# Attention outputs leave their PSUM bank in one copy and are added when the rows are loaded; seven bias tables are added up on GpSimd

## The chip, the cores and the metric

The kernel runs on one core of one Trainium2 chip. Its time is the device time of one execution in microseconds. Three runs of the kernel before took 1325.66 to 1327.61 us, median 1326.53 us. A further execution was recorded by the hardware profiler; all lines of the profile come from that one. The engines are named as the profile names them: PE (TensorE, with PEld for its weight loads), DVE (VectorE), ACT (ScalarE), POOL (GpSimd) and SP (SyncE, whose queue issues the DMAs).

## The reference

One layer of an encoder on 1024 tokens of 1024 features, in float32:

```
h = rms_norm(x) ; q_a,k_a,v_a, q_b,k_b,v_b, g_a,g_b = split(h @ w_in)
o_a = neighbourhood_attention(norm(q_a), norm(k_a), v_a, rpb)   # 8 heads of 64, 8 x 16 window of a 16 x 64 grid, bias by relative place
o_b = sliding_window_attention(norm(q_b), norm(k_b), v_b, sink, t5)  # 8 heads, 2 key heads, +-128 tokens
y = sigmoid(g_a) * (o_a @ w_branch_a) + sigmoid(g_b) * (o_b @ w_branch_b)
x = x + y @ w_out
x = x + (silu(rms_norm(x) @ w_gate) * (rms_norm(x) @ w_up)) @ w_down      # 2816 hidden
```

## The kernel before

Every operand of a product is split into a high part that TensorE's fp32r type holds and the low part that is left. A product is then three matmuls (high by high, high by low, low by high). The helper `split` makes the parts: ScalarE copies the high part (L50), VectorE, or at some weights GpSimd, subtracts it from the source (L51; L54 where a scale goes in).

**Stages.** The projections of the first group of heads end at about 53 us of the span. Attention follows until about 398 us, then eight pairs of gate products (`gate_pair`, `Seven`) until about 524 us, then the two branch products with the sigmoids of the gates until about 611 us, then the output product and the feed-forward part.

**Attention.** There are 16 heads with 8 blocks of 128 queries each. They come in groups, two neighbourhood heads (`na`) or four sliding-window heads (`sw`): na, sw, na, sw, na, na. A loop of steps (L722 to L742) gives TensorE, for one block after another: `scores` (matmuls into a bank `s`, L592 and L593), three steps later `flip` (three transposes into a bank `t`, L616), five steps later `values` (L654). Between them go "filler" products that other stages need: the projections of the next groups (`pj`, L325 to L327) and the first gates (`pg`, L427 to L429). The order of TensorE's instructions is written out by hand.

In `scores`, VectorE adds the bias table to the scores and reduces them to their maximum (L598), ScalarE takes exponentials and their sum (L604), VectorE the reciprocal (L605), and GpSimd multiplies (L606); the result is the tile `E`. In `flip`, the transposed weights `tp` are split into `ph` (ScalarE, L50) and `pl` (VectorE, L51). In `values`, TensorE multiplies `ph` and `pl` by a tile that holds, for one head, 64 columns of the high part of the values and 64 of the low part. The result has 128 rows: 64 of one part and 64 of the other. Their sum is the head's output. It stands in the bank `o`, of which there is one (`BANKS`, L39), for half of the tokens at a time. So the product of the next half can begin only when the last half has been read out of the bank.

`store_half` (L623) reads it out: ScalarE copies 64 of the rows to the tile `of` (L636), VectorE adds the other 64 rows to them (L637). Two heads share one `of` of 128 rows, which goes to DRAM in one DMA (L640). There are 32 halves, so 32 copies, 32 adds, and 8 stores of 512 KB.

`bias_table` adds a head's relative biases (`brna`) to the window's mask (`bna`), in two adds of 128x384 for each na head (L570, VectorE). It is called two steps ahead of the head's first block, that is at the seventh block of the head before. The first head's table is made in the opening.

**Beside attention.** `row_sums` prepares operands for the gates (`ta`, `tb`, `hs`: L503, L507, L511, L515, L51, L54) during the last heads. Its instructions are held behind the instruction in `att["bound"]`, which is the latest reduction of scores (L598).

**The rows for the branch products.** `load_o` (L924 to L928) loads four tiles of 128 rows and 512 tokens from `o_dram`, one DMA each, and splits each into its parts. It is called four times, at steps of the gates 5 and 7: rows 4 to 7, first half; rows 0 to 3, first half; rows 4 to 7, second half; rows 0 to 3, second half. The first gates' values (`load_sg`) are loaded ahead of the last of these. In the turns of the branch products each pair of gates goes through a sigmoid (L993), then `product` of the weights `wb` with rows 4 to 7, then with rows 0 to 3, into banks `pb`.

**Who sets the order.** TensorE's order is the program's. The DMAs that go through `dma` (L95) keep the order of the program on SP's queue. Apart from the opening, the instructions of ScalarE, VectorE, GpSimd and the other DMAs are ordered by a scheduler.

Of the kernel before, what the change touches and what calls it, by code (L numbers as in the profile page):

```python
# [25 lines left out]
def block_kernel(ctx, tc, x, xt, small, w_in, rpb, t5, w_ba, w_bb, w_out, w_gate, w_up, w_down,  # L26
                 onehot, swmask, namask, out):
    nc = tc.nc
    P = 128
# [15 lines left out]
    def f(ap):  # L45
        return ap.bitcast(F32)

    def split(hi, lo, src, eng=None, scale=None):
        if scale is None:
            a = nc.scalar.copy(hi, src)  # L50
            b = (eng or nc.vector).tensor_tensor(lo, src, f(hi), ALU.subtract)  # L51
        else:
            a = nc.scalar.activation(hi, src, AF.Copy, scale=scale)
            b = nc.vector.scalar_tensor_tensor(lo, src, scale, f(hi), op0=ALU.mult, op1=ALU.subtract)  # L54
        return a.ins, b.ins
# [31 lines left out]
    def half_cols(h):  # L87
        return slice(h * 512, h * 512 + 512)
# [6 lines left out]
    def dma(dst, src):  # L95

        tc.keep_in_program_order(nc.sync.dma_start(dst, src))
# [4 lines left out]
    def tok(t):  # L102
        return slice(t * P, (t + 1) * P)
# [68 lines left out]
    load_small()  # L172
    load_x(0, 0, 0)

    o_dram = drp.tile([8 * P, T], F32, name="o_dram")
    swe = drp.tile([8, 512], F32, name="swe")
    nae = drp.tile([64, 744], F32, name="nae")
    g_dram = drp.tile([32 * P, 512], F32, name="g_dram")
# [47 lines left out]
    att = {}  # L226
# [205 lines left out]
    def run(gen):  # L432
        for _ in gen:
            pass
# [94 lines left out]
    with tc.tile_pool(name="at", bufs=1) as ap:  # L529
# [34 lines left out]
        def bias_table(hd):  # L564
            bt = hd["table"]
            if hd["kind"] == "sw":
                return lambda qb: bt[:, 128:384] if qb == 0 else (bt[:, 0:256] if qb == 7 else bt[:, 0:384])
            v = hd["raw"].rearrange("p (a d b) -> p d a b", a=16, d=3)
            for o in (0, 384):
                ins = nc.vector.tensor_add(  # L570
                    bt[:, o:o + 384].rearrange("p (d a b) -> p d a b", d=3, a=16), v,
                    bt[:, o:o + 384].rearrange("p (d a b) -> p d a b", d=3, a=16))
# [9 lines left out]
        of_tiles = {}  # L582

        def scores(hd, qb):
            q, k1, k2, v = groups[hd["gi"]]
# [23 lines left out]
        def flip(hd, kb):  # L609
            q0, q1 = max(0, kb - 1), min(7, kb + 1)  # L610
            n = (q1 - q0 + 1) * P
            nm_ = f"{hd['gi']}_{hd['hl']}_{kb}"
            tp = bank("t", "tp" + nm_)
            for j, qq in enumerate(range(q0, q1 + 1)):
                ko = (kb - max(0, qq - 1)) * P
                nc.tensor.transpose(tp[:, tok(j)], hd["E"][qq][:, ko:ko + P], ident)  # L616
            ph = ap.tile([P, 384], F32R, tag="ph", name="ph" + nm_, bufs=4)
            pl = ap.tile([P, 384], F32R, tag="pl", name="pl" + nm_, bufs=4)
            split(*(z[:, :n].rearrange("p (j i) -> p j i", i=P) for z in (ph, pl)),
                  tp[:, :n].rearrange("p (j i) -> p j i", i=P)[:, :, ::-1])  # L620
            hd["P"][kb] = (ph, pl)

        def store_half(hd, half):  # L623
            gi, e = hd["gi"], hd["hl"] % 2
            pair = (gi, hd["hl"] // 2)
            if pair not in of_tiles:
                of_tiles[pair] = ap.tile([P, T], F32, tag="of", name=f"of{gi}_{hd['hl']}", bufs=1)
            of = of_tiles[pair]
            own, oth = slice(e * HD, e * HD + HD), slice(HD - e * HD, 2 * HD - e * HD)
            O = hd["O"][half]  # L630
            if hd["kind"] == "na":
                dst, sh = of[own, half_cols(half)], lambda z: z
            else:
                dst = of[own, :].rearrange("p (s r c) -> p r s c", r=16, s=8)[:, 8 * half:8 * half + 8]
                sh = lambda z: z.rearrange("p (r s c) -> p r s c", r=8, s=8)
            nc.scalar.copy(dst, sh(O[oth, :]))  # L636
            nc.vector.tensor_add(dst, sh(O[own, :]), dst)  # L637
            if e == 1 and half == 1:
                row = ((0 if hd["kind"] == "na" else 4) + hd["h"] // 2) * P
                nc.sync.dma_start(o_dram[row:row + P, :], of)  # L640

        def values(hd, block):

# [115 lines left out]
    def scratch(nm):  # L759
        return hp.tile([P, 512], F32, tag="S", name=nm, bufs=2)  # L760
# [35 lines left out]
    class Seven:  # L796
# [27 lines left out]
        def step(self, p, rows=None):  # L824

            hi, lo = self.prepare(p)
            z = {1: "X", 2: "X", 5: "V", 6: "Z" if self.early else "Y", 3: "Y"}.get(p, "Z")
            ps = self.banks[z]
            for j in range(self.n) if rows is None else rows:
                bh, bl = self.mv[p][j]  # L830
                first, end = j == 0 and (p in (1, 5) or self.early and p == 3), j == self.n - 1
                nc.tensor.matmul(ps, hi[:, tok(j)], bh, start=first, stop=False, skip_group_check=True)  # L832
                nc.tensor.matmul(ps, hi[:, tok(j)], bl, start=False, stop=False, skip_group_check=True)  # L833
                nc.tensor.matmul(ps, lo[:, tok(j)], bh, start=False, stop=end, skip_group_check=True)  # L834
            if p == 1 or p == 6 and not self.early:
                nc.scalar.copy(self.banks["Z" if self.early or p == 6 else "Y"], ps)

    class TokenSums(dict):

# [84 lines left out]
    def load_o(r0, half):  # L924
        for r in range(r0, r0 + 4):
            o_rows[r, half] = hi, lo = operand("H", f"o{r}_{half}")
            dma(f(lo), o_dram[tok(r), half_cols(half)])
            split(hi, lo, f(lo))  # L928


    wb, sgs = {}, {}
# [11 lines left out]
    def load_sg(d, half):  # L943
        for br in (1, 0):
            z = sgs[d, half, br] = weight_sum(f"sg{d}_{half}_{br}")
            dma(z, gate_rows(d, br, half))
# [16 lines left out]
        load_branch(1)  # L963
        load_o(4, 1)

    def behind_three():
        load_sg(0, 0)
        load_o(0, 1)

    run(gate_pair(7, ORDER, {6: lambda: load_o(0, 0), 2: behind_two, 3: behind_three}))  # L970

    sets = bank_sets()
    my = {}
# [2 lines left out]
    def out_loads(i):  # L976
# [3 lines left out]
                w_out[0, :, tok(2 * i + a)].rearrange("(k p) c -> p k c", p=P))  # L980
        return Seven(f"o{i}", [two(z) for z in st], 4, my, sets)

    turns = [(2 * j + e, half) for j in range(4) for half in range(2) for e in range(2)]
# [535 lines left out]
```

## Time and profile before

| | |
|---|---|
| median of three runs | 1326.53 us (1325.66 to 1327.61) |
| the profiled execution | 1324.66 us |
| its span, first to last instruction | 1322.9 us |
| around the span | 1.76 us |
| PE busy | 1306.8 us (99%), 6618 matmuls |
| DVE, ACT, POOL busy | 1037.3 us (78%), 699.3 us (53%), 172.4 us (13%) |
| granted clock | 1.000 |
| DMA | 183.52 MB, 139 GB/s on average |

A row of the timeline gives the start in the span, the duration, the engine, the line, the operation, what it writes and reads, its shape, and in brackets how long the engine was idle before it and who released it. Instructions of an engine overlap a little: on VectorE the next one begins some 0.08 us before the last ends. A row of the waits gives who waited for whom, how long in total, how often, and the longest. The names leave out the buffers' numbers.

### The profile page before, as it was taken

Reading aid. Unit: us, or ns where it says so; the run is one execution under the profiler, and the core shown is the slowest. Engines: PE = TensorE matmul, PEld = TensorE weight load, DVE = VectorE, ACT = ScalarE, POOL = GpSimd, SP = SyncE. Lnnn points to the kernel's source line nnn. Section 1 sums busy time; section 2 is a strip of 40 time slices with the busy share of each in tenths; the row PEclk is TensorE's granted clock in tenths of the full one; section 3 lists DMA queues with packets and bytes.
Section 4 is the critical chain, followed back from the end, with each engine's and each line's share of the span. In section 5 each row is a group of like instructions: output and inputs, shape, how many; then the busy total and the mean of one; then the engine's idle time right before and its main releaser. Section 6 shows DMA issues by size and latency. Waiting matters only on the chain.

```text
span 1322.9 us, 19555 instructions
## 1 busy us (share of the span) xinstructions
PE 1306.8 (99%) x6618; PEld 1133.3 (86%) x6618; DVE 1037.3 (78%) x2069; ACT 699.3 (53%) x1459; POOL 172.4 (13%) x308
## 2 busy tenths in 40 slices
PE   9999999999999999999999999999999999999998
PEld 8999999999878788888887888888888888888887
DVE  5678878887787756778899887887777789798764
ACT  6667857786663334536457544434444456363532
POOL 1364645454220000000000000000000000000000
PEclk9999999999999999999999999999999999999999
DMA  9531313141424345748684532333333346672532
GB/s 311 145 88 40 92 51 94 45 118 51 130 88 167 116 138 166 250 145 259 203 290 120 159 112 80 98 118 100 92 112 119 121 167 215 239 255 64 178 129 83
DMA packets 177284, 183.52 MB, mean 139 GB/s; under 512 B 20464, under 2 KB 125936, under 8 KB 177184
## 3 DMA queue, kind: packets, MB, share of 16 engines
q1 hardware_dynamic: 176928, 182.18, 43.8%
q8 instruction: 52, 0.85, 0.3%
q14 instruction: 48, 0.39, 0.1%
q10 hardware_dynamic: 256, 0.10, 0.0%
HBM read 129.00 MB, written 48.18 MB: 134 GB/s over the span
## 4 chain that ended last, share of the span: by engine, by line
PE 84%; DVE 6%; DMA 4%; ACT 3%; issue 2%; POOL 1%; SPq 0%; ACTq 0%; DVEq 0%; POOLq 0%
PE bankZ L832 5%; PE bankZ L833 5%; PE bankZ L834 5%; PE bankY L833 5%; PE bankY L832 5%; PE bankY L834 5%; PE bankX L832 4%; PE bankX L834 4%; PE bankX L833 4%; PE pj L327 4%; PE pj L325 4%; PE pj L326 4%; PE bankV L833 3%; PE bankV L832 3%; PE bankV L834 3%; PE o L654 3%
## 5 line engine op out<-in xcount | busy, mean ns | idle before, releaser
L604 ACT ACTIVATE E<-E,nm 128x384 f32<-128x384 f32 (+3 forms) x128 | 75.7, 591 | 48.7 <-DVE nm L598 42.9
L606 POOL TENSOR_SCALAR E<-E,nm 128x384 f32<-128x384 f32 (+1 forms) x128 | 78.9, 617 | 103.8 <-DVE nm L605 72.3
L51 DVE TENSOR_TENSOR pl<-tp,ph 128x384 fp32r<-128x384 f32 (+1 forms) x128 | 66.3, 518 | 10.6 <-ACT ph L50 9.4
L50 ACT CAST ph<-tp 128x384 fp32r<-128x384 f32 (+1 forms) x128 | 57.4, 448 | 20.7 <-PE tp L616 19.6
L50 ACT CAST f<-f 128x512 fp32r<-128x512 f32 x87 | 51.3, 619 | 27.4 <-DMA f<-u_dram 22.4
L51 DVE TENSOR_TENSOR f<-f 128x512 fp32r<-128x512 f32 x87 | 56.5, 686 | 8.8 <-ACT f L50 8.7
L616 PE MATMUL tp<-ident,E 128*128 128x128 f32 x352 | 59.6, 273 | 0.1
L654 PE MATMUL o<-pl,v 128*128 128x256 f32 (+2 forms) x160 | 49.2, 308 | 4.0 <-DVE pl L51 3.9
L616 PEld LDWEIGHTS tp<-ident,E 128*128 128x128 f32 x352 | 45.2, 140 | 5.2 <-POOL E L606 0.3
L345 POOL TENSOR_TENSOR ss<-ss,mhalf 128x4 f32<-128x4 f32 (+2 forms) x42 | 49.1, 1170 | 3.1
L654 PE MATMUL o<-ph,v 128*128 128x256 f32 (+2 forms) x160 | 46.2, 303 | 3.2 <-DVE of L637 3.2
L592 PE MATMUL s<-k,q 128*128 128x384 f32 (+1 forms) x128 | 46.4, 363 | 0.0
L1213 POOL TENSOR_TENSOR rs<-rs,mhalf 128x4 f32<-128x4 f32 x2 | 2.9, 1444 | 321.5 <-DVE rs L1212 321.5
L593 PE MATMUL s<-k,q 128*128 128x384 f32 (+1 forms) x128 | 41.3, 323 | 0.0
L598 DVE CUSTOM_DVE_ANT_0 E<-s,bsw,cols 128x384 f32<-128x384 f32 (+1 forms) x64 | 36.8, 576 | 2.7 <-PE s L593 2.0
L1230 ACT ACTIVATE u<-u 128x512 f32<-128x512 f32 x44 | 27.7, 630 | 19.8 <-DVE u L1229 19.8
L598 DVE CUSTOM_DVE_ANT_0 E<-s,bna 128x384 f32<-128x384 f32 (+1 forms) x64 | 33.1, 517 | 4.8 <-PE s L593 4.2
L605 DVE RECIPROCAL nm<-nm 128x1 f32<-128x1 f32 x128 | 20.2, 159 | 21.1 <-ACT E L604 19.7
L1231 DVE TENSOR_TENSOR u<-u,wide_rs 128x512 f32<-128x512 f32 x44 | 30.2, 689 | 7.4 <-ACT u L1230 6.6
L654 PEld LDWEIGHTS o<-pl,v 128*128 128x128 f32 x160 | 30.1, 188 | 6.8 <-DVE pl L51 6.1
L833 PE MATMUL bankV<-f,f_5h 128*128 128x512 f32 x88 | 34.5, 392 | 1.0 <-DVE f L54 1.0
L654 PEld LDWEIGHTS o<-ph,v 128*128 128x128 f32 x160 | 30.1, 188 | 6.1 <-DVE of L637 5.3
(1266 smaller groups left out, 4650.7 us busy)
## 6 DMA issues: line engine op xcount, KB each, us to landing
f<-u_dram SPq DMA_DIRECT2D x77, 256.0 KB
wg_s<-in_w_gate_dram SPq DMA_DIRECT2D x22, 512.0 KB
u_dram<-u SPq DMA_DIRECT2D x33, 256.0 KB
sg<-g_dram SPq DMA_DIRECT2D x32, 256.0 KB
g_dram<-go SPq DMA_DIRECT2D x24, 256.0 KB
u_dram<-tau SPq DMA_DIRECT2D x22, 256.0 KB
u_dram<-tbu SPq DMA_DIRECT2D x22, 256.0 KB
rows<-in_x_dram SPq DMA_DIRECT2D x8, 512.0 KB
```

Of the source, the lines that this page charges most:

```text
L50: a = nc.scalar.copy(hi, src)
L51: b = (eng or nc.vector).tensor_tensor(lo, src, f(hi), ALU.subtract)
L325: nc.tensor.matmul(ps[:, :384], lh, his[k][:, :384], start=(k == 0), stop=False)
L326: nc.tensor.matmul(ps[:, :384], lh, los[k][:, :384], start=False, stop=False)
L598: att["bound"] = nc.vector.tensor_tensor_reduce(E[:, :n], s[:, :n], hd["bias"](qb), -1.0, sk if sw else 1e30, ALU.add, ALU.min, nm[:, 0:1] ...
L604: nc.scalar.activation(E[:, :m], E[:, :m], AF.Exp, bias=nm[:, 0:1], scale=-1.0, accum_out=nm[:, 1:2])
L606: nc.gpsimd.tensor_scalar(E[:, :n], E[:, :n], nm[:, 1:2], 1.0, op0=ALU.mult, op1=ALU.mult)
L616: nc.tensor.transpose(tp[:, tok(j)], hd["E"][qq][:, ko:ko + P], ident)
L654: nc.tensor.matmul(hd["O"][half][:, (a - half * 4) * P:(z + 1 - half * 4) * P], v[:, kb].rearrange("p a e -> p (a e)"), pp[:, (a - q0) * P ...
L832: nc.tensor.matmul(ps, hi[:, tok(j)], bh, start=first, stop=False, skip_group_check=True)
L833: nc.tensor.matmul(ps, hi[:, tok(j)], bl, start=False, stop=False, skip_group_check=True)
L834: nc.tensor.matmul(ps, lo[:, tok(j)], bh, start=False, stop=end, skip_group_check=True)
```

## The change

`store_half` has ScalarE copy all 128 rows of the bank to a tile `of` of the head's own. The 32 adds on VectorE are gone. Each head is stored by itself, so there are 16 stores of 512 KB, and `o_dram` has twice the rows. `load_o` loads each row tile in two DMAs, one for each part of two heads' outputs, adds them on VectorE into a scratch tile `os`, and splits that: 16 more loads of 256 KB and 16 adds. The bias tables of all na heads but the first are added on GpSimd. `att["bound"]` is VectorE's half of the flip's split. The first gates are loaded at step 1 of gate pair 7 instead of step 3, and the sigmoids are held behind the last copy between banks in gate pair 7.

```diff
-    o_dram = drp.tile([8 * P, T], F32, name="o_dram")
+    o_dram = drp.tile([16 * P, T], F32, name="o_dram")
...
-                ins = nc.vector.tensor_add(
+                ins = (nc.gpsimd if hd is not heads[0] else nc.vector).tensor_tensor(
                     bt[:, o:o + 384].rearrange("p (d a b) -> p d a b", d=3, a=16), v,
-                    bt[:, o:o + 384].rearrange("p (d a b) -> p d a b", d=3, a=16))
+                    bt[:, o:o + 384].rearrange("p (d a b) -> p d a b", d=3, a=16), ALU.add)
...
-            split(*(z[:, :n].rearrange("p (j i) -> p j i", i=P) for z in (ph, pl)),
-                  tp[:, :n].rearrange("p (j i) -> p j i", i=P)[:, :, ::-1])
+            _, att["bound"] = split(*(z[:, :n].rearrange("p (j i) -> p j i", i=P) for z in (ph, pl)),
+                                    tp[:, :n].rearrange("p (j i) -> p j i", i=P)[:, :, ::-1])
...
-            nc.scalar.copy(dst, sh(O[oth, :]))
-            nc.vector.tensor_add(dst, sh(O[own, :]), dst)
-            if e == 1 and half == 1:
-                row = ((0 if hd["kind"] == "na" else 4) + hd["h"] // 2) * P
-                nc.sync.dma_start(o_dram[row:row + P, :], of)
+            if not half:
+                hd["of"] = ap.tile([P, T], F32, tag="of", name=f"of{hd['gi']}_{hd['hl']}", bufs=1)
+            of, O = hd["of"], hd["O"][half]
+            if hd["kind"] == "na":
+                nc.scalar.copy(of[:, half_cols(half)], O)
+            else:
+                nc.scalar.copy(of.rearrange("p (s r c) -> p r s c", r=16, s=8)[:, 8 * half:8 * half + 8],
+                               O.rearrange("p (r s c) -> p r s c", r=8, s=8))
+            if half:
+                nc.sync.dma_start(o_dram[tok((0 if hd["kind"] == "na" else 8) + hd["h"]), :], of)
...
-            dma(f(lo), o_dram[tok(r), half_cols(half)])
-            split(hi, lo, f(lo))
+            for z, row in ((hi, 0), (lo, HD)):
+                src = o_dram[2 * r * P + row:2 * r * P + row + 1, half_cols(half)]
+                dma(f(z), bass.AP(src.tensor, src.offset, [[P * T, 2], [T, HD], [1, 512]]))
+            both = scratch(f"os{r}_{half}")
+            nc.vector.tensor_tensor(both, f(hi), f(lo), ALU.add)
+            split(hi, lo, both)
...
-    def behind_three():
-        load_sg(0, 0)
-        load_o(0, 1)
-
-    run(gate_pair(7, ORDER, {6: lambda: load_o(0, 0), 2: behind_two, 3: behind_three}))
+    run(gate_pair(7, ORDER, {1: lambda: load_sg(0, 0), 6: lambda: load_o(0, 0), 2: behind_two, 3: lambda: load_o(0, 1)}))
...
-            nc.scalar.activation(sg, sg, AF.Sigmoid)
+            with tc.issue_after(last_copy):
+                nc.scalar.activation(sg, sg, AF.Sigmoid)
```

TensorE's matmuls stand in the same order as before. On the other engines the order is another at many places; three of them follow. In the rows, `E4_1_6` is the weights tile of group 4, head 1, block 6, and `nm` its scale.

GpSimd's queue at the end of the second head of group 4, before:

```order
L606 TENSOR_SCALAR E4_1_5_4899<-E4_1_5_4899,nm4_1_5_4900 128x384
L606 TENSOR_SCALAR E4_1_6_4941<-E4_1_6_4941,nm4_1_6_4942 128x384
L606 TENSOR_SCALAR E4_1_7_4965<-E4_1_7_4965,nm4_1_7_4966 128x256
L606 TENSOR_SCALAR E5_0_0_4984<-E5_0_0_4984,nm5_0_0_4985 128x256
L606 TENSOR_SCALAR E5_0_1_5009<-E5_0_1_5009,nm5_0_1_5010 128x384
```

and now (line 605 is the old 606):

```order
L605 TENSOR_SCALAR E4_1_5_4886<-E4_1_5_4886,nm4_1_5_4887 128x384
L605 TENSOR_SCALAR E4_1_6_4928<-E4_1_6_4928,nm4_1_6_4929 128x384
L570 TENSOR_TENSOR bna6_4672<-brna6_4673,bna6_4672 128x384 x2
L605 TENSOR_SCALAR E4_1_7_4952<-E4_1_7_4952,nm4_1_7_4953 128x256
L605 TENSOR_SCALAR E5_0_0_4971<-E5_0_0_4971,nm5_0_0_4972 128x256
L605 TENSOR_SCALAR E5_0_1_4996<-E5_0_1_4996,nm5_0_1_4997 128x384
```

The next head's table stands between the normalisations of the last two blocks.

VectorE's queue at the same place, before (L278 makes the normalised `q` of the next group, L598 is the reduction of scores):

```order
L570 TENSOR_TENSOR bna6_4684<-brna6_4685,bna6_4684 128x384 x2
L51 TENSOR_TENSOR pl4_1_3_4959<-tp4_1_3_4954,ph4_1_3_4958 128x384
L278 SCALAR_TENSOR_TENSOR q5_1_4028<-tq5_4_0_4929,cols_81,q5_1_4028 64x512
L598 ISA E5_0_0_4984,nm5_0_0_4985<-s5_0_0_4981,bna6_4684 128x256
L598 ISA nm5_0_0_4985 128x1
L605 RECIPROCAL nm4_1_7_4966<-nm4_1_7_4966 128x1
L51 TENSOR_TENSOR pl4_1_4_4978<-tp4_1_4_4973,ph4_1_4_4977 128x384
```

and now (L597 is the old 598, L604 the old 605):

```order
L51 TENSOR_TENSOR pl4_1_3_4946<-tp4_1_3_4941,ph4_1_3_4945 128x384
L278 SCALAR_TENSOR_TENSOR q5_1_4018<-tq5_4_0_4916,cols_81,q5_1_4018 64x512
L604 RECIPROCAL nm4_1_7_4953<-nm4_1_7_4953 128x1
L51 TENSOR_TENSOR pl4_1_4_4965<-tp4_1_4_4960,ph4_1_4_4964 128x384
L597 ISA E5_0_0_4971,nm5_0_0_4972<-s5_0_0_4968,bna6_4672 128x256
L597 ISA nm5_0_0_4972 128x1
```

The table pair is gone, and the split `pl4_1_4` stands ahead of the first reduction that reads the new table.

VectorE's queue at the end of attention, in the last head (group 5, head 1), before:

```order
L454 TENSOR_TENSOR graw0_0_0_5453<-pg0_0_0_5324,wide_rs0_110 128x512
L54 SCALAR_TENSOR_TENSOR hs5_1_5477<-ta1_5460,cols_81,hs5_1_5477 128x512
L51 TENSOR_TENSOR pl5_1_4_5437<-tp5_1_4_5432,ph5_1_4_5436 128x384
L515 SCALAR_TENSOR_TENSOR tb1_5461<-xo1_5379,cols_81,ta1_5460 128x512
L51 TENSOR_TENSOR hs7_1_5523<-tb1_5461,hs7_1_5523 128x512
L51 TENSOR_TENSOR hs6_1_5499<-ta1_5460,hs6_1_5499 128x512
L51 TENSOR_TENSOR pl5_1_5_5471<-tp5_1_5_5466,ph5_1_5_5470 128x384
```

and now:

```order
L454 TENSOR_TENSOR graw0_0_0_5438<-pg0_0_0_5309,wide_rs0_110 128x512
L51 TENSOR_TENSOR pl5_1_4_5422<-tp5_1_4_5417,ph5_1_4_5421 128x384
L503 TENSOR_TENSOR ta1_5445<-xe1_5363 128x512
L51 TENSOR_TENSOR pl5_1_5_5456<-tp5_1_5_5451,ph5_1_5_5455 128x384
L507 SCALAR_TENSOR_TENSOR ta1_5445<-ta1_5445,cols_81,g22h_5210 128x512
L54 SCALAR_TENSOR_TENSOR hs5_1_5462<-ta1_5445,cols_81,hs5_1_5462 128x512
```

The splits `pl5_1_4` and `pl5_1_5` stand ahead of the row sums that they stood behind.

More of the change, by code (lines that the diff above doesn't have):

```diff
@@ L581, in block_kernel @@
                       for hl in range(nq)]
-        of_tiles = {}
         def scores(hd, qb):
@@ L618, in flip @@
             pl = ap.tile([P, 384], F32R, tag="pl", name="pl" + nm_, bufs=4)
-            split(*(z[:, :n].rearrange("p (j i) -> p j i", i=P) for z in (ph, pl)),
-                  tp[:, :n].rearrange("p (j i) -> p j i", i=P)[:, :, ::-1])
+            _, att["bound"] = split(*(z[:, :n].rearrange("p (j i) -> p j i", i=P) for z in (ph, pl)),
+                                    tp[:, :n].rearrange("p (j i) -> p j i", i=P)[:, :, ::-1])
             hd["P"][kb] = (ph, pl)
         def store_half(hd, half):
[L624 to L630, printed above, removed]
+            if not half:
+                hd["of"] = ap.tile([P, T], F32, tag="of", name=f"of{hd['gi']}_{hd['hl']}", bufs=1)
+            of, O = hd["of"], hd["O"][half]
             if hd["kind"] == "na":
-                dst, sh = of[own, half_cols(half)], lambda z: z
+                nc.scalar.copy(of[:, half_cols(half)], O)
             else:
[L634 to L637, printed above, removed]
-            if e == 1 and half == 1:
-                row = ((0 if hd["kind"] == "na" else 4) + hd["h"] // 2) * P
-                nc.sync.dma_start(o_dram[row:row + P, :], of)
+                nc.scalar.copy(of.rearrange("p (s r c) -> p r s c", r=16, s=8)[:, 8 * half:8 * half + 8],
+                               O.rearrange("p (r s c) -> p r s c", r=8, s=8))
+            if half:
+                nc.sync.dma_start(o_dram[tok((0 if hd["kind"] == "na" else 8) + hd["h"]), :], of)
         def values(hd, block):
@@ L835, in step @@
             if p == 1 or p == 6 and not self.early:
-                nc.scalar.copy(self.banks["Z" if self.early or p == 6 else "Y"], ps)
+                self.copied = nc.scalar.copy(self.banks["Z" if self.early or p == 6 else "Y"], ps).ins
     class TokenSums(dict):
@@ L981, in out_loads @@
         return Seven(f"o{i}", [two(z) for z in st], 4, my, sets)
+    last_copy = pairs[7].copied
     turns = [(2 * j + e, half) for j in range(4) for half in range(2) for e in range(2)]
```

## The prediction

> **What bounds the kernel now.** I read the page's head first, then a table of windows by stage, then TensorE's waits, then the timeline at the longest of them. The head and the windows (columns: length, then PE, PEld, DVE, ACT and POOL busy):
>
> ```profile
> span 1322.9 us, 19555 instructions
> ...
> PE 1306.8 (99%) x6618; PEld 1133.3 (86%) x6618; DVE 1037.3 (78%) x2069; ACT 699.3 (53%) x1459; POOL 172.4 (13%) x308
> ...
> 53.00:398.00 345.00, 336.00 (x2105) 318.64 (x2104) 277.45 (x794) 240.07 (x623) 159.33 (x288) 1.00 0.28 80
> ...
> 524.00:611.00 87.00, 87.00 (x385) 72.05 (x384) 65.85 (x102) 45.02 (x74) 0.00 (x0) 1.00 0.71 226
> ```
>
> TensorE is the bound: 1306.8 of 1322.9 us, at a granted clock of 1.00. The change gives it the same products in the same order, so it can win only from the 16.1 us in which TensorE stands. Attention (53 to 398 us) holds 345.00 - 336.00 = 9.0 of them; the branch products (524 to 611 us) hold none, so there any new wait is pure loss. Who makes TensorE wait (total, times, longest):
>
> ```profile
> PE o L654 <- DVE pl L51: 3.9, 6, 1.0
> PE o L654 <- DVE of L637: 3.2, 6, 1.1
> ...
> PE tq L299 <- DVE q L278: 0.7, 1, 0.7
> ```
>
> 7.8 of the 9.0 us are VectorE arriving late: 3.2 because the add L637 still reads the one O bank into which the next half is to be summed, 3.9 because the low part of the turned weights (pl) is late, 0.7 for a turned q. The change takes work off VectorE at these places.
>
> **Term 1, the O bank: -3.2 us.** The longest wait, and the one with the least room behind it:
>
> ```profile
> 353.70 0.58 ACT L636 COPY of<-o 64x512 f32<-64x512 f32 x1
> ...
> 355.43 0.69 DVE L637 TENSOR_TENSOR of<-o,of 64x512 f32<-64x512 f32 x1
> ...
> 356.17 0.33 PE L654 MATMUL o<-ph,v 128*128 128x128 f32 x1 [1.06 <-DVE of L637]
> ```
> ```profile
> 158.80 0.58 ACT L636 COPY of<-o 64x512 f32<-64x512 f32 x1
> ...
> 159.41 0.68 DVE L637 TENSOR_TENSOR of<-o,of 64x512 f32<-64x512 f32 x1
> ...
> 160.15 0.33 PE L654 MATMUL o<-ph,v 128*128 128x128 f32 x1 [0.25 <-DVE of L637]
> ```
>
> ScalarE is done with the bank at 354.28, TensorE stands from 356.17 - 1.06 = 355.11, and VectorE lets go only at 356.12. In the second place the same three times are 159.38, 159.90 and 160.09. With the copy as the only reader the bank is free 0.5 to 0.8 us before TensorE wants it, and all six waits go. The copy takes 128 rows in place of 64, with 512 elements in each as before; I take its 0.58 us unchanged. Bounds: 0.58 to 1.16 if rows counted; at 1.16 the first bank is still free in time, at 354.86, the second at 159.96 (0.06 late). So -3.1 to -3.2.
>
> **Term 2, late pl: -2.8 of 3.9 us.** Three of the six, each behind a different kind of work:
>
> ```profile
> 167.82 0.67 DVE L637 TENSOR_TENSOR of<-o,of 64x512 f32<-64x512 f32 x1
> 168.42 0.54 DVE L51 TENSOR_TENSOR pl<-tp,ph 128x384 fp32r<-128x384 f32 x1
> ...
> 170.36 0.56 DVE L51 TENSOR_TENSOR pl<-tp,ph 128x384 fp32r<-128x384 f32 x1
> ...
> 170.97 0.44 PE L654 MATMUL o<-pl,v 128*128 128x384 f32 x1 [0.78 <-DVE pl L51]
> ...
> 348.85 1.00 DVE L570 TENSOR_TENSOR bna<-brna,bna 128x384 f32<-128x384 f32 x2
> ...
> 349.10 1.13 POOL L606 TENSOR_SCALAR E<-E,nm 128x384 f32<-128x384 f32 x1 [2.45 <-PE s L593]
> ...
> 349.78 0.55 DVE L51 TENSOR_TENSOR pl<-tp,ph 128x384 fp32r<-128x384 f32 x1
> ...
> 350.38 0.39 PE L654 MATMUL o<-pl,v 128*128 128x256 f32 x1 [0.46 <-DVE pl L51]
> ...
> 388.57 0.73 DVE L54 SCALAR_TENSOR_TENSOR hs<-ta,cols,hs 128x512 fp32r<-128x512 f32 x1
> 389.23 0.54 DVE L51 TENSOR_TENSOR pl<-tp,ph 128x384 fp32r<-128x384 f32 x1
> ...
> 389.83 0.33 PE L654 MATMUL o<-pl,v 128*128 128x128 f32 x1 [0.97 <-DVE pl L51]
> ```
>
> At 170 an add L637 stands in the VectorE queue ahead; without it all behind moves up by 0.60 (the next instruction starts at 168.42): -0.60. At 350 the 0.93 us from the table pair's start to pl's goes to GpSimd: the whole 0.46. At 389 the row sums' hs (388.57 to 389.23) now stands behind pl: -0.66 of 0.97. The other three waits hold 3.9 - 0.78 - 0.46 - 0.97 = 1.7; I credit as large a share as these three give, 1.72 of 2.21, less a little: -1.1. Sum -2.8, between -1.7 (nothing for the other three) and -3.9.
>
> **Term 3, the turned q: -0.6 us.**
>
> ```profile
> 100.77 0.68 DVE L637 TENSOR_TENSOR of<-o,of 64x512 f32<-64x512 f32 x1
> ...
> 102.84 0.41 PE L299 MATMUL tq<-ident,qn 128*128 128x128 f32 x2 [0.70 <-DVE q L278]
> ```
>
> TensorE waits for VectorE's L278, which stands in VectorE's queue behind this add. Such an add holds the queue for 0.60 us (167.82 to 168.42 above), and without it 0.1 of 0.7 is left. Bounds 0 and -0.7.
>
> **What is added.** GpSimd gets seven tables. The nearest row is its two-input subtraction of the same 128x384, beside VectorE's row for the table itself:
>
> ```profile
> L51 POOL TENSOR_TENSOR wg_1l<-wg_0s,wg_1h 128x384 fp32r<-128x384 f32 x4 | 4.1, 1014 | 0.0
> ...
> L51 POOL TENSOR_TENSOR wg_7l<-wg_3s,wg_7h 128x384 fp32r<-128x384 f32 x4 | 4.4, 1111 | 1.1 <-ACT wg_7h L50 1.0
> ...
> L570 DVE TENSOR_TENSOR bna<-brna,bna x16: 537/548/703, 53.5 to 367.4; 128x384 f32<-128x384 f32 x16
> ...
> 346.06 0.59 POOL L606 TENSOR_SCALAR E<-E,nm 128x384 f32<-128x384 f32 x1 [6.30 <-DVE nm L605]
> ...
> 351.14 0.42 DVE L598 CUSTOM_DVE_ANT_0 E<-s,bna 128x256 f32<-128x256 f32 x1
> ...
> 351.82 0.48 POOL L606 TENSOR_SCALAR E<-E,nm 128x256 f32<-128x256 f32 x1 [1.59 <-PE tp L616]
> ...
> 352.74 0.27 PE L654 MATMUL o<-pl,v 128*128 128x128 f32 x1
> 352.86 0.51 PE L616 MATMUL tp<-ident,E 128*128 128x128 f32 x3
> ```
>
> So 2 x 1.01 = 2.0 us a table, by the row with nothing beside it. The far ends are 1.1 (VectorE's price) and 4.4 (twice 2 x 1.11, since a table reads runs of 8 elements, which no GpSimd row shows). The Trainium skill's GPSIMD Engine Reference, section 3, calls GpSimd the wrong engine for elementwise adds, 1.96 times as slow as VectorE; by that rule the 14 adds should stay on VectorE, and the sum would lack a table's gain and charge, about -6.1. 1014 over 548 ns is 1.85: the trace bears the factor out. But GpSimd is busy 13% of the span, and what decides is the gap behind a head's seventh block: the normalisation there takes 0.59 instead of 1.13 us once VectorE's pair is gone, the table runs from 349.7 to 351.7, the last block's normalisation is wanted from 351.82, and the transpose that reads it, the third of the three that begin at 352.86, starts about 353.1. GpSimd fits, with 0.8 us over. VectorE's next score reduction (351.14) waits 0.6 us for the table, and what is queued behind it waits too; but the split of the pl that TensorE wants first, at 352.74, has been put ahead of this reduction. I charge no more than one new wait of the present mean size, 3.9 / 6 = 0.65, for such a delay: **+0.65** (0 to 2). The same page (section 1, SBUF interfaces) says the two engines contend when VectorE reads two operands in SBUF. The rows agree: 1.13 us of normalisation beside L570, 0.59 without; now a VectorE split of weights may lose some 0.2 us beside a table, off the path.
>
> The stores double to 16 of 512 KB. Each waits for its copy alone and holds `of` until the next head's first copy, half a head later; I cost them at nothing. The loads double too:
>
> ```profile
> 526.13 0.91 SPq L97 DMA_DIRECT2D sg<-g_dram  x2
> 527.14 1.80 SPq L97 DMA_DIRECT2D o<-o_dram  x4
> ...
> 532.21 0.69 DVE L51 TENSOR_TENSOR o<-o 128x512 fp32r<-128x512 f32 x1 [1.80 <-ACT o L50]
> ...
> 536.00 0.69 DVE L51 TENSOR_TENSOR o<-o 128x512 fp32r<-128x512 f32 x1
> ...
> 540.07 0.39 PE L427 MATMUL pb<-o,wb00h 128*128 128x512 f32 x1
> ```
>
> This last set (rows 0 to 3, second half) is the tightest. Its last row is ready at 536.69 and wanted at 540.07: 3.4 us of cover. Eight issues take 3.6 us instead of 1.8, but the two gate loads ahead of them (0.91) now go earlier: 0.9 late. Four more adds of 0.60 us are 2.4 if none finds a gap. Together 0.9 to 3.3 of 3.4 us, so nothing reaches TensorE. The sigmoids behind the last bank copy wait for gates that lie ready; no cost seen.
>
> **The sum.** -3.2 - 2.8 - 0.6 + 0.65 = -5.95. The profiled execution, 1324.66 us (span 1322.9 and 1.76 around it), becomes 1318.7. It lies 1.87 us under the median of the three runs, 1326.53; the same step from there gives **1320.6 us**. Own range 1318.7 (all 7.8 us of the three lines, nothing new) to 1322.9 (terms 2 and 3 at -1.7 and 0, two new waits).
>
> **Rivals.**
> *The pl waits come back, 1323.3.* TensorE that no longer stands for the bank arrives earlier at each pl; then only term 1 lasts, -3.2. For it: VectorE is busy 277 of 345 us there, so the queue is rarely empty. Against: 32 adds and 14 table adds, about 32 x 0.60 + 14 x 0.5 = 26 us, leave that queue in this stage. Chance 0.14.
> *The rows come late, 1323.5 to 1326.* The second half's extra 1 MB at this stage's 226 GB/s is 4.6 us of transfer; if it all lies behind the old loads, the last row loses up to 0.9 + 4.6 of the 3.4 us of cover, plus adds that find no gap: TensorE waits 2 to 4.5 at 540. Against: the transfers of a row's two parts run beside each other. 0.12.
> *GpSimd's tables are slow, about 1331.* The last block's normalisation is late once a table takes over 353.1 - 0.48 - 349.7 = 2.9 us, 1.46 per add; with each of seven heads as here, 5.95 / 7 = 0.85 us more (1.9 per add) eats the gain, and at 2.2 per add it is 7 x 1.5 - 5.95 = +4.5. For it: the short runs. Against: both 128x384 rows, at 1.01 and 1.11. 0.07. (The warning of the Trainium skill's GPSIMD Engine Reference, section 3, weighed above, points this way; no run yet shows a table there.)
> *The release isn't what TensorE waited for, 1326.5.* Should another reader or the product's other operands come as late, nothing changes. Against: in both quoted places the product starts 0.05 to 0.06 us behind the add. 0.04.
>
> **How the numbers follow.** The forecast has 0.63. What a measurement can tell from no change is 0.2%, 2.65 us. Faster: 0.63, 0.09 of the first rival, 0.05 of the second: 0.77. Slower: 0.07. Within: 0.16. The range 1318.0 to 1325.0 starts some 0.7 under the own range, about the runs' own spread (1325.66 to 1327.61), and leaves out the last two rivals and half of the second.
>
> **What would show it.** Right: TensorE's waits list has no line for the O bank's release, pl's line is 0.6 to 1.7 us, attention's window holds 2 to 4 us of idle, a table pair on GpSimd takes 2.0 us, and branch products stay without idle. Wrong: waits of the transposes on GpSimd's E, of scores' reduction chains at heads' ends over 1 us, of pb on o at 540, or pl still near 3.9.

## The result

The changed kernel takes 1455.95 us (median of four runs, 1452.78 to 1456.43) against 1326.1 us before: a ratio of 1.098, 95% interval [1.0957, 1.1003]. The forecast was 1320.6 us, faster. It is wrong in sign and by 135 us. The profiled execution took 1456.43 us, its span 1454.6 us.

The head of the changed kernel's page: busy time of the engines, and from the 40 slices of the span TensorE's busy share, the granted clock in tenths and the DMA engines' busy share.

```profile
span 1454.6 us, 19602 instructions
...
PE 1321.9 (91%) x6618; PEld 1142.1 (79%) x6618; DVE 1020.9 (70%) x2039; ACT 696.7 (48%) x1459; POOL 181.8 (12%) x322
...
PE   9999999999999373316999999999999999999998
...
PEclk9999999999999786657999999999999999999999
DMA  9331432324543221116477734333333337654442
```

The loss sits in slices 14 to 19. There TensorE stands, the DMA engines are hardly busy (1 or 2 tenths until the last of these slices), and the granted clock falls. TensorE's idle time is 132.7 us in place of 16.1, which is 116.6 us more. Its busy time is 15.1 us longer for the same 6618 matmuls. Together that is the span's 131.7 us.

The same windows of time as before, now in the changed kernel (length, PE, PEld, DVE, ACT and POOL busy, clock, DMA share, GB/s). From the second on they no longer hold the same work: the last row tile is added at 666 us, and the branch products end at 742 us in place of 611.

```profile
53.00:398.00 345.00, 342.05 (x2144) 326.39 (x2143) 257.36 (x757) 238.01 (x625) 168.77 (x302) 1.00 0.33 99
398.00:524.00 126.00, 97.46 (x417) 79.53 (x415) 62.92 (x100) 33.16 (x58) 0.00 (x0) 0.89 0.30 99
524.00:611.00 87.00, 41.62 (x148) 31.37 (x148) 24.46 (x39) 14.02 (x23) 0.00 (x0) 0.73 0.21 75
```

Attention has 2.95 us of idle in place of 9.0. The 6 us that the forecast spoke of are there. What follows attention loses some 122 us, twenty times as much, to the first four of these waits (the fifth is attention's):

```profile
PE pb L428 <- DVE o L51: 65.4, 8, 10.0
PE bankZ L825 <- ACT bankZ L829: 26.5, 1, 26.5
PE bankZ L825 <- DVE gp L891: 25.6, 2, 22.7
PE pb L427 <- ACT o L50: 4.2, 2, 2.8
PE o L647 <- DVE pl L51: 2.2, 4, 0.7
```

Two of the four name the rows `o`. The other two name a copy of ScalarE and an add of VectorE that have nothing to do with the rows. The timelines of SP, VectorE and ScalarE in the gates show what those two had to wait for:

```profile
477.42 28.92 SPq L97 DMA_DIRECT2D o<-o_dram  x8
```
```profile
490.87 0.69 DVE L924 TENSOR_TENSOR os<-o 128x512 f32<-128x512 f32 x1 [13.88 <-DMA o<-o_dram]
...
501.29 0.69 DVE L924 TENSOR_TENSOR os<-o 128x512 f32<-128x512 f32 x1 [8.36 <-DMA o<-o_dram]
...
511.76 0.69 DVE L924 TENSOR_TENSOR os<-o 128x512 f32<-128x512 f32 x1 [9.78 <-DMA o<-o_dram]
```
```profile
512.49 0.62 ACT L50 CAST o<-os 128x512 fp32r<-128x512 f32 x1 [9.85 <-DVE os L924]
513.01 0.58 ACT L829 COPY bankZ<-bankY 128x512 f32<-128x512 f32 x1
```
```profile
513.64 0.80 PE L825 MATMUL bankZ<-hs,g_7h 128*128 128x512 f32 x1 [26.51 <-ACT bankZ L829]
```
```profile
567.98 0.69 DVE L924 TENSOR_TENSOR os<-o 128x512 f32<-128x512 f32 x1 [9.77 <-DMA o<-o_dram]
568.59 0.68 DVE L891 TENSOR_TENSOR gp<-bankZ,gp 128x512 f32<-128x512 f32 x1
```

A row tile arrives every 10.4 us (490.87, 501.29, 511.76). VectorE's add waits for it, ScalarE's cast waits for the add, and the copy of the gate's bank stands in ScalarE's queue behind that cast. So TensorE waits 26.5 us for a copy of 0.58 us. The sums of the gates (L891) wait the same way in VectorE's queue: the one at 568.59 comes right behind an add that waited for its rows, and TensorE has then stood 22.7 us for it.

A row tile is two loads of 256 KB, so a load takes 5.2 us: 50 GB/s. The DMA view of this window has one digit and one rate per slice. For the changed kernel, 478 to 500 us:

```profile
DMA  9200111111111111111111111111111111111111
GB/s 358 15 11 26 30 48 52 52 52 52 52 48 48 52 52 52 52 52 48 52 48 52 52 48 48 52 52 48 48 52 52 48 48 52 52 48 48 52 52 48
```

From 484 to 500 us the busy share of the 16 DMA engines is 0.13, which is 2.1 of 16. The new load reads `[[P * T, 2], [T, HD], [1, 512]]`: its outermost dimension, the first pair in this list of steps and counts, counts the two heads.

### The profile page after: what moved, and what is told of

Its sections match the earlier page's. It is cut to its first block, busy times and chain, and to the rows that moved or that the text cites. A ratio compares the mean times of both kernels' runs of the same rounds, so it can differ in the third digit from the quotient of the medians.

```text
span 1454.6 us, 19602 instructions
## 1 busy us (share of the span) xinstructions
PE 1321.9 (91%) x6618; PEld 1142.1 (79%) x6618; DVE 1020.9 (70%) x2039; ACT 696.7 (48%) x1459; POOL 181.8 (12%) x322
## 4 chain that ended last, share of the span: by engine, by line
PE 75%; DMA 10%; DVE 7%; SPq 5%; ACT 2%; issue 1%; POOL 1%; ACTq 0%; DVEq 0%; POOLq 0%
DMA o<-o_dram 5%; PE bankZ L825 5%; PE bankZ L826 5%; PE bankZ L827 5%; PE bankY L825 5%; PE bankY L826 5%; PE bankY L827 5%; SPq L97 4%; PE bankX L827 4%; PE bankX L825 4%; PE bankX L826 4%; PE pj L327 4%; PE pj L325 4%; PE pj L326 4%; PE o L647 3%; PE bankV L826 2%
## 5 line engine op out<-in xcount | busy, mean ns | idle before, releaser
L924 DVE TENSOR_TENSOR os<-o 128x512 f32<-128x512 f32 x16 | 11.1, 692 | 144.3 <-DMA o<-o_dram 144.3
L605 POOL TENSOR_SCALAR E<-E,nm 128x384 f32<-128x384 f32 (+1 forms) x128 | 74.7, 585 | 95.0 <-DVE nm L604 78.4
L50 ACT CAST o<-os 128x512 fp32r<-128x512 f32 x16 | 9.9, 616 | 134.7 <-DVE os L924 134.7
L604 DVE RECIPROCAL nm<-nm 128x1 f32<-128x1 f32 x128 | 20.4, 160 | 29.4 <-ACT E L603 27.9
L597 DVE CUSTOM_DVE_ANT_0 E<-s,bsw,cols 128x384 f32<-128x384 f32 (+1 forms) x64 | 36.9, 576 | 3.5 <-PE s L592 2.8
L428 PE MATMUL pb<-o,wb10h 128*128 128x512 f32 x8 | 4.8, 595 | 37.5 <-DVE o L51 37.5
L597 DVE CUSTOM_DVE_ANT_0 E<-s,bna 128x384 f32<-128x384 f32 (+1 forms) x64 | 33.1, 518 | 8.0 <-PE s L592 5.2
```

The source lines that it names most:

```text
L597: att["bound"] = nc.vector.tensor_tensor_reduce(E[:, :n], s[:, :n], hd["bias"](qb), -1.0, sk if sw else 1e30, ALU.add, ALU.min, nm[:, 0:1] ...
L605: nc.gpsimd.tensor_scalar(E[:, :n], E[:, :n], nm[:, 1:2], 1.0, op0=ALU.mult, op1=ALU.mult)
```

## The experiments

Theory: the count of a load's outermost dimension sets how many of the 16 DMA engines it uses, so the new loads run on two. Rivals: twice the bytes and loads, or rows that are fetched from places apart, are slow as such. Times are medians, and each is compared with runs of the kernel before on the same chip.

**The same loads, 128 rows flat (e1_flat).** The layout in DRAM is another, so that a part of two heads is 128 rows in a row.

```diff
-                nc.sync.dma_start(o_dram[tok((0 if hd["kind"] == "na" else 8) + hd["h"]), :], of)
+                pair, e = divmod((0 if hd["kind"] == "na" else 8) + hd["h"], 2)
+                for part in range(2):
+                    row = (2 * pair + part) * P + e * HD
+                    nc.sync.dma_start(o_dram[row:row + HD, :], of[part * HD:part * HD + HD, :])
...
-            for z, row in ((hi, 0), (lo, HD)):
-                src = o_dram[2 * r * P + row:2 * r * P + row + 1, half_cols(half)]
-                dma(f(z), bass.AP(src.tensor, src.offset, [[P * T, 2], [T, HD], [1, 512]]))
+            for part, z in enumerate((hi, lo)):
+                dma(f(z), o_dram[tok(2 * r + part), half_cols(half)])
```

> The changed kernel with another layout in DRAM: the two heads' first parts stand in 128 rows behind each other, then their second parts, so that each load of a row tile is a plain one of 128 rows; each store is two of 64 rows. The order on TensorE, VectorE, ScalarE and GpSimd is nearly the changed kernel's. Theory (a load whose outermost dimension counts 2 uses 2 of the 16 DMA engines): loads at full width again, no wait of pb on o, attention's gain of some 6 us left over: 1318.5 to 1323 us, against 1326 of the kernel before. Rival (twice the bytes, read back in more pieces, are the cost): above 1400 us, since bytes and number of loads are the same.

It took 1321.36 us against 1324.41: ratio 0.9975 [0.9964, 0.9987]. The whole loss is gone and a gain is left, with the same number of loads and bytes. TensorE's list has no wait for the rows, and the branch products stand at 87.00 of 87.00 us busy. Of the rivals, bytes and number of loads are out. Attention keeps less of its gain than in the changed kernel, 339.12 against 342.05 us busy: there are twice as many stores, and the scheduler places a few of VectorE's instructions otherwise. Which of the two it is was not tried. The trace points to the stores: two of them, in place of one, stand on SP's queue right ahead of the loads of `xe` and `xo` for the row sums, and ScalarE waits 3.1 us for `xo`, where the changed kernel has no such wait.

**The same rows from the same places, in loads of 64 rows (e2_split).**

```diff
-                src = o_dram[2 * r * P + row:2 * r * P + row + 1, half_cols(half)]
-                dma(f(z), bass.AP(src.tensor, src.offset, [[P * T, 2], [T, HD], [1, 512]]))
+                for e in range(2):
+                    at = (2 * r + e) * P + row
+                    dma(f(z)[e * HD:e * HD + HD, :], o_dram[at:at + HD, half_cols(half)])
```

> The changed kernel with its layout and the same rows read, but each load of 2 x 64 rows issued as two loads of 64 rows. Theory (outermost dimension of 2): loads at full width, 1319 to 1326 us, the upper end if 64 issues of some 0.45 us delay the last set. Rival (rows fetched from two places a head apart are slow to read): as the changed kernel, near 1455 us.

One run: 1323.48 us. The places apart are out as well. Attention keeps 341.90 of 345.00 us busy. TensorE waits 2.8 us for rows at the branch products (2.3 on ScalarE's part and 0.5 on VectorE's), while SP issues 16 loads in 10.0 us. These short waits come with a slower clock:

```profile
531.14 0.79 PE L428 MATMUL pb<-o,wb00h 128*128 128x512 f32 x1 [0.22 <-DVE o L51]
...
534.93 0.80 PE L427 MATMUL pb<-o,wb00h 128*128 128x512 f32 x1 [0.54 <-ACT o L50]
```

None is longer than 1.4 us, yet from 534 to 538 us the granted clock is 0.50, and matmuls take 0.80 us in place of 0.39. TensorE's busy time is 1308.5 us against 1305.0 in e1_flat's profile and 1306.8 before, so the late rows may have taken back some 4.5 to 6.3 us (an estimate: 2.8, and 1.7 to 3.5 of busy time), most of what attention gains.

**The dose (e3_outer4, e9_outer8, e10_outer16).** e1_flat with another order of the source's rows, in groups of every fourth (shown), eighth and sixteenth row.

```diff
-                dma(f(z), o_dram[tok(2 * r + part), half_cols(half)])
+                src = o_dram[tok(2 * r + part), half_cols(half)][0:1, :]
+                dma(f(z), bass.AP(src.tensor, src.offset, [[T, 4], [4 * T, P // 4], [1, 512]]))
```

> As e1_flat, but each load's source goes in 4 groups of 32 rows, every fourth row (the rows of a tile come out permuted, so the output is not the reference's). Theory: 4 of 16 DMA engines, so 100 GB/s and 2.6 us per 256 KB in place of 5.2; 32 loads take 84 us in place of 167, of which some 50 to 60 lie under the gates: 1340 to 1370 us. Rival (anything but the outermost count): as e1_flat, near 1321 us.

> As e3_outer4, with 8 groups of 16 rows, every eighth row (rows permuted, output not the reference's). Theory: 8 of 16 DMA engines, 200 GB/s while a load is alone, 1.3 us per 256 KB, 32 loads in 42 us: nearly all under the gates, 1321 to 1326 us. Rival (any source whose rows don't follow each other is slow): near e3_outer4, 1380 us.

> As e3_outer4, with 16 groups of 8 rows, every sixteenth row (rows permuted, output not the reference's). Theory: all 16 DMA engines, so as e1_flat, 1320 to 1323 us. Rival (any source whose rows don't follow each other is slow): near e3_outer4, 1380 us.

They took 1380.48, 1335.91 and 1326.01 us (one run each). The DMA view from 478 to 500 us, for a count of 4, then 8, then 16:

```profile
GB/s 344 309 289 332 289 11 0 276 201 19 365 108 60 48 71 97 104 104 104 97 104 101 101 101 86 97 101 101 104 101 97 101 104 101 101 104 101 101 97 104
```
```profile
GB/s 311 295 323 328 26 0 164 313 0 272 205 130 93 209 164 149 127 115 134 201 201 205 197 205 201 209 201 205 197 205 209 190 67 0 0 0 0 82 346 164
```
```profile
GB/s 187 203 296 344 319 307 300 352 194 0 19 369 89 119 354 101 253 264 283 242 250 182 197 287 339 276 268 272 276 227 78 22 0 0 0 0 0 153 324 201
```

Where the loads run alone the rate is 50 at a count of 2, 101 at 4 and 205 at 8, about 25 GB/s for each of the outermost dimension's items. The busy share of the 16 DMA engines there is 0.13, 0.26 (486.5 to 500 us) and 0.52 (488.5 to 495.5 us), which is 2, 4 and 8 of 16. At 16 the share is 0.93 (486.5 to 492.5 us), at 252 GB/s. That is the theory's dose, and rows out of order cost little by themselves: the 16 has the most scattered rows of the three and the shortest time. The times of the first two were forecast too low (1340 to 1370, 1321 to 1326). I had counted the loads' own time, not the copies and sums of the gates that queue up behind each late tile, nor the clock: TensorE's busy time is 13.6 and 5.1 us longer than in e1_flat. The 16 missed its forecast too (1320 to 1323). Of its 5.4 us above e1_flat's profiled execution (1320.62) the trace shows a part: TensorE waits 3.5 us for ScalarE's bank copies in the gates, where e1_flat waits 0.8. The rest, from single runs on two chips, stays open.

The Trainium skill's DMA: Bandwidth & Descriptors has this rule, in the section on why a DMA increments its semaphore by 16: a copy goes to the largest number of engines, up to 16, that divides the slowest dimension of both access patterns. It gives 2, 4, 8 and 16 here, and the busy shares of the engines agree (0.13, 0.26, 0.52, 0.93). The prediction did not weigh it.

**The outermost 2 alone, in the kernel before (e4_before_outer2).**

```diff
-            dma(f(lo), o_dram[tok(r), half_cols(half)])
+            src = o_dram[tok(r), half_cols(half)][0:1, :]
+            dma(f(lo), bass.AP(src.tensor, src.offset, [[T, 2], [2 * T, HD], [1, 512]]))
```

> The kernel before with one change: each of its 16 row loads takes the even rows, then the odd rows, so its outermost dimension counts 2 (rows permuted, so the output is not the reference's). Bytes, number of loads and adds are the old ones. Theory: 16 x 5.2 = 84 us of loading, of which some 50 to 60 lie under the gates: 1345 to 1375 us. Rival (the doubled loads and their adds are the cost): 1326 us as before.

It took 1389.31 us, 65 more than before (one run), with neither a new add nor a byte more. TensorE's longest waits are of the same kinds as in the changed kernel:

```profile
PE bankZ L832 <- ACT bankZ L836: 31.5, 2, 16.5
PE pb L427 <- ACT o L50: 19.9, 6, 5.8
```

The rows' order is the only other thing that changed, and e10_outer16 shows that a more scattered order has no such price. So the cause is shown by itself, and the size was forecast too low for the reasons just named.

**What the other parts are worth.** Three kernels are e1_flat with parts undone, two are the kernel before with parts added. The edits: the tables' engine (`nc.gpsimd` or `nc.vector` in L570), the bound (`_, att["bound"] = split(...)` or the reduction's), and for the third the old places of `load_sg` and of the sigmoids as well.

```diff
 e5_dve_tables, e7_copy_only:
-                ins = (nc.gpsimd if hd is not heads[0] else nc.vector).tensor_tensor(
+                ins = nc.vector.tensor_tensor(
 e6_old_bound, e7_copy_only:
-            _, att["bound"] = split(*(z[:, :n].rearrange("p (j i) -> p j i", i=P) for z in (ph, pl)),
+            split(*(z[:, :n].rearrange("p (j i) -> p j i", i=P) for z in (ph, pl)),
```

> e1_flat with the seven bias tables back on VectorE. The prediction's step (the table pair holds up pl by 0.46 us at 350, and GpSimd has room): 0.5 to 1.5 us longer than e1_flat's 1321.4. Rival (the tables on GpSimd cost what they save, by the waits of the last block's transposes and of VectorE's reductions): equal to e1_flat or up to 1 us shorter.

> e1_flat with the row sums bound to the reduction of scores again, as in the kernel before. The prediction's step: a pl of the last head waits behind the row sums again, 0.7 to 1.0 us longer than e1_flat. Rival (the row sums only push the wait elsewhere, into the gates): equal within 0.3 us.

> e1_flat with all else undone: tables on VectorE, the old bound, the gates' loads and sigmoids as before. Left are the copy of the whole bank, the flat loads and the adds of the rows. The prediction's steps: term 1 (3.2 us), the 0.6 us of the add at 170 and its like, and the 0.6 us of q: 3.2 to 5 us shorter than the kernel before. Rival (the pl waits take back what the bank's release gives): within 1.5 us of the kernel before.

> The kernel before with one change: the seven bias tables on GpSimd. The prediction's step: 0.5 to 1 us shorter than the kernel before. Rival (GpSimd's tables are too slow for the gap behind the seventh block): 0.5 us or more longer.

> The kernel before with the seven tables on GpSimd and the row sums bound to the split of pl, without the copy of the whole bank and without anything at the rows. If the wait for the O bank is worth its 3.2 us only together with the bound, this stays 1.5 to 3 us below the kernel before (the tables' 1.8 and some of the 1.0 of pl at 389), that is 1321.5 to 1323.5. Rival (the bound is what gains, not the bank): 4 us or more below, 1320.5 or less.

| kernel | us | ratio to before | attention busy of 345.00 us |
|---|---|---|---|
| before | | | 336.00 |
| changed | 1455.95 | 1.098 [1.0957, 1.1003] | 342.05 |
| e1_flat | 1321.36 | 0.9975 [0.9964, 0.9987] | 339.12 |
| e5_dve_tables | 1324.38 | 1.0000 [0.9990, 1.0009] | 337.57 |
| e6_old_bound | 1324.83 | 0.9999 [0.9989, 1.0008] | 337.02 |
| e7_copy_only | 1330.1 | 1.0042 [1.0027, 1.0057] | 335.98 |
| e8_tables_only | 1322.91 | 0.9984 [0.9975, 0.9994] | 337.64 |
| e12_tables_bound | 1323.12 | 0.9989 [0.9980, 0.9999] | 338.15 |

Tables on GpSimd gain with the copy (e1_flat against e5) and without it (e8): 1.6 us of attention both times. Their rival is out. The bound is worth 2.1 us of attention with the copy (e1_flat against e6) and 0.5 without (e12 against e8). The 0.5 is no finding: attention as it stands in the kernel before is busy 336.00 us in one profile and 335.62 in another (e4_before_outer2). In whole time e5 and e6 lie 3.0 and 3.5 us above e1_flat, more than their forecasts (0.5 to 1.5, 0.7 to 1.0); what lies outside attention was not followed. e8 gains 1.8 where 0.5 to 1 was forecast. e12 came out as forecast, so the bound alone is not what gains.

The great miss is e7_copy_only: the copy without the other parts was to gain 3.2 to 5 us, and it loses 5.4 (against 1324.7). The bank's waits are gone, but in place of pl's 3.9 us the list has this:

```profile
PE o L650 <- DVE pl L51: 5.8, 8, 2.5
PE bankX L828 <- ACT bankZ L832: 2.0, 1, 2.0
PE pb L428 <- DVE o L51: 1.5, 3, 0.8
...
PE o L650 <- ACT ph L50: 1.4, 1, 1.4
```

The longest of these, in e7_copy_only's timelines of ScalarE, VectorE and TensorE:

```profile
385.91 0.72 ACT L502 ACTIVATE g22h<-xo,cols 128x512 f32<-128x512 f32 x1 [2.54 <-DMA xo<-in_xt_dram]
386.54 0.70 ACT L53 ACTIVATE hs<-ta,cols 128x512 fp32r<-128x512 f32 x1
387.15 0.45 ACT L50 CAST ph<-tp 128x384 fp32r<-128x384 f32 x1
```
```profile
389.25 0.74 DVE L515 SCALAR_TENSOR_TENSOR tb<-xo,cols,ta 128x512 f32<-128x512 f32 x1
389.92 0.55 DVE L51 TENSOR_TENSOR pl<-tp,ph 128x384 fp32r<-128x384 f32 x1
```
```profile
387.66 0.33 PE L650 MATMUL o<-ph,v 128*128 128x128 f32 x1 [1.35 <-ACT ph L50]
390.52 0.47 PE L650 MATMUL o<-pl,v 128*128 128x128 f32 x1 [2.54 <-DVE pl L51]
```

With the old bound the row sums stand ahead of `ph` and `pl`, and they wait for the load of `xo`. So 3.3 us come back as waits for `ph` and `pl`, and attention ends where it was (335.98 against 336.00). But the wait for `xo` need not be the copy's doing. ScalarE waits 4.4 us for `xo` here and 3.1 to 3.7 in the other kernels with e1_flat's 32 stores, 0.4 to 1.9 in the kernel before and its variants, and none in the changed kernel, e2_split and e11_two_queues, which have the copy with 16 stores. The copy alone with 16 stores was not run. What it is worth on top of tables and bound can be read: 342.05 - 338.15 = 3.9 us of attention with 16 stores (the changed kernel against e12), 339.12 - 338.15 = 1.0 with 32. (These are single profiles; the two above of the same attention differ by 0.4.) Outside attention, e7_copy_only's gates hold 3.0 us of idle and its branch products 1.5, in place of 0.15 and none. The places of the first gates' loads and of the sigmoids were not tried by themselves.

**Half of the loads on ScalarE's queue (e11_two_queues).** e2_split with every second load issued by ScalarE.

```diff
-                    dma(f(z)[e * HD:e * HD + HD, :], o_dram[at:at + HD, half_cols(half)])
+                    tc.keep_in_program_order((nc.sync if e else nc.scalar).dma_start(
+                        f(z)[e * HD:e * HD + HD, :], o_dram[at:at + HD, half_cols(half)]))
```

> e2_split with half of its 64 row loads issued by ScalarE instead of SP. In e2_split attention kept the whole 6 us and the gates lost nothing, but TensorE waited 2.8 us for rows, behind 64 issues on one queue. If the issues were what made the rows late, those 2.8 us go: 1318.5 to 1321 us, the changed kernel's idea at the price that was forecast for it. Rival (the doubled bytes or VectorE's adds made them late): as e2_split, 1323.5 us.

It took 1353.11 us: ratio 1.0212 [1.0196, 1.0227]. Both sides missed. ScalarE's timeline shows why:

```profile
510.77 0.62 ACT L50 CAST o<-os 128x512 fp32r<-128x512 f32 x1 [0.98 <-DVE os L926]
510.78 1.21 ACTq L923 DMA_DIRECT2D o<-o_dram  x2
515.21 0.62 ACT L50 CAST o<-os 128x512 fp32r<-128x512 f32 x1 [3.81 <-DVE os L926]
515.22 1.10 ACTq L923 DMA_DIRECT2D o<-o_dram  x2
520.29 0.62 ACT L50 CAST o<-os 128x512 fp32r<-128x512 f32 x1 [4.46 <-DVE os L926]
```

The next tile's loads stand in ScalarE's queue behind the cast of the tile before, which waits for its own load. The tiles come one at a time, 4.4 and 5.1 us apart, and TensorE waits 23.6 us for the rows. That does not tell whether SP's issues were what made e2_split's rows late.

The best version of all runs is e1_flat, 0.25% below the kernel before.

## Why the prediction was wrong

*The loads of the rows: the step that failed.* "Eight issues take 3.6 us instead of 1.8" and "so nothing reaches TensorE". I priced a new load by the issue and landing of the old one, as if 256 KB were 256 KB. Eight issues took 28.9 us in the gates, a tile 10.4 us. e4_before_outer2 and the dose show that the outermost count of the load's address list does it. The rival "the rows come late" had the place (TensorE at `pb` on `o`) and a wrong price, 2 to 4.5 us for some 122 of waits, because it went by this stage's 226 GB/s, where the new loads moved 50. (Its time is also added up wrongly: 1320.6 + 2 to 4.5 is 1322.6 to 1325.1, not 1323.5 to 1326.) It also looked at `pb` alone. The in-order queues of ScalarE and VectorE carried the delay into the gates, which don't read rows at all (52 us of the waits).

*The clock.* Not foreseen: in the two windows in which TensorE stands, the granted clock is 0.89 and 0.73, and a matmul of 0.39 us takes 0.80. TensorE's busy time grows by 15.1 of the 131.7 us.

*Term 1, the bank, -3.2 us: right.* All six waits are gone, and with the changed kernel's 16 stores the copy is worth 3.9 us of attention on top of tables and bound (the forecast for bank and q was 3.8). With 32 stores it is worth 1.0 there and nothing in e7_copy_only. There `pl` waits come back, as the rival with a chance of 0.14 said, but the longest by another way than the rival's: the row sums wait for `xo`.

*Term 2, pl, -2.8 us: -1.7 measured.* The waits at 350 (table) and 389 (row sums) are gone, as worked out. That is 1.43 for these two, where 0.46 + 0.66 was counted. The other four, 0.27, 0.78, 0.69 and 0.72, are still 0.24, 0.72, 0.55 and 0.71: 0.24 less, where 0.60 + 1.1 was counted. The wrong step is "without it all behind moves up by 0.60", taken as 0.60 less of wait. In the kernel before, and then in the changed one, TensorE's rows of the 0.78 are:

```profile
168.05 0.34 PE L593 MATMUL s<-k,q 128*128 128x384 f32 x1
168.55 0.39 PE L654 MATMUL o<-ph,v 128*128 128x256 f32 x1 [0.16 <-DVE of L637]
```
```profile
166.68 0.34 PE L592 MATMUL s<-k,q 128*128 128x384 f32 x1
166.86 0.28 PE L647 MATMUL o<-ph,v 128*128 128x256 f32 x1
...
169.10 0.44 PE L647 MATMUL o<-pl,v 128*128 128x384 f32 x1 [0.72 <-DVE pl L51]
```

and VectorE's in the changed kernel:

```profile
167.06 0.61 DVE L597 CUSTOM_DVE_ANT_0 E<-s,bsw,cols 128x384 f32<-128x384 f32 x1
...
167.72 0.74 DVE L278 SCALAR_TENSOR_TENSOR q<-tq,cols,q 64x512 fp32r<-64x512 f32 x1
168.49 0.56 DVE L51 TENSOR_TENSOR pl<-tp,ph 128x384 fp32r<-128x384 f32 x1
```

From the scores' start (166.68) to pl's start are 1.81 us; before, from 168.05 (same matmul) to 170.36, they were 2.31. VectorE gained 0.50. But TensorE's stop comes 1.70 us behind the same scores and not 2.14, so 0.44 of it is lost again. Most of that, 0.32, lies between the two matmuls shown: 0.50 us before, with a wait for the bank, and 0.18 now. So at this place terms 1 and 2 counted the same gain twice. At the other three the add began 3.1 to 7.6 us ahead of the pl in VectorE's queue, with reductions and `q` of L278 between, which stay.

*Term 3, q, -0.6: right.* The 0.7 of tq are gone, and 0.4 of a wait for qn at 100 that I had not counted.

*The tables: right.* A pair takes 1.98 to 1.99 us on GpSimd, between 1.1 and 4.4, at the forecast 2.0, and no wait of TensorE names them; the +0.65 did not come. The sum for attention, -5.95, was measured as 342.05 - 336.00 = 6.05 us: right, but in part by luck, because 1.1 us too much at pl, 0.65 that did not come and 0.5 at q and qn cancel.

```profile
346.03 1.99 POOL L570 TENSOR_TENSOR bna<-brna,bna 128x384 f32<-128x384 f32 x2
347.99 0.49 POOL L605 TENSOR_SCALAR E<-E,nm 128x256 f32<-128x256 f32 x1
```

## What to carry to other kernels

In these runs a DMA had to be priced by the steps and counts of its address list before its bytes: where a changed load's outermost dimension is no longer the 128 rows, take its rate from a load of the same form, or change the layout at the store so that the load stays flat. A late load costs not only its reader but everything queued behind the engine that waits for it, so look for what stands in order behind the first instruction that uses it. And a wait that is taken away makes TensorE earlier at the next one: add such gains up only after asking whether the next producer moves too.

## What the runs showed of the hardware

A load on SP's queue ran at 50, 101 and 205 GB/s with an outermost count of 2, 4 and 8, about 25 GB/s per item, at busy shares of 0.13, 0.26 and 0.52 of the 16 DMA engines. GpSimd's add over runs of 8 elements took 1014 ns per 128x384 (median of 14, 1007 to 1024), the same as its contiguous subtraction (1014). ScalarE's copy out of a PSUM bank took 0.59 us for 128 rows and 0.58 for 64. In the changed kernel the granted clock was 0.73 on average from 524 to 611 us, where TensorE was busy for 41.62 of 87.00 us, and single matmuls of 128x512 took 0.80 instead of 0.39 us. In e2_split waits of at most 1.4 us, 2.8 in sum, went with a clock of 0.50 from 534 to 538 us.
